# A two-layer decoder trunk on one core: gated GEMM steps and RWKV chain batches tied in turn, a first norm from raw rows, group-norm turns moved later

## The chip, the cores and the metric

The kernel runs on one core of a Trainium2 chip. The metric is the device time of one execution in microseconds (us), as the median of several runs. The engines are named as in the profile: PE is TensorE (PEld its weight loads), DVE VectorE, ACT ScalarE, POOL GpSimd, and SP the engine that here issues nearly all the weight DMAs.

## The reference

Two layers on 256 tokens of width 1024. Each layer is a half-step SwiGLU FFN (inner width 2816), two mixers side by side with gates, and a second half-step FFN; a last RMS norm ends it. Cut to what the change touches:

```python
for layer in range(2):
    x = x + 0.5 * swiglu_ffn(rms_norm(x, ffn1_norm[layer]), ...)
    h = rms_norm(x, mix_norm[layer])
    p = h @ w_in
    y_a = chunked_sgu(...)                    # gMLP spatial gating
    # RWKV-7, per head and token t (64x64 state):
    #   sa = state @ kk_t
    #   state = state * w_t - sa (kk_t a_t)^T + v_t k_t^T
    #   y_t = state @ r_t, then group norm per head, gain, bias, + bonus
    y_b = rwkv7_time_mix(...)
    merged = sigmoid(gate_a) * (y_a @ w_proj_a) + sigmoid(gate_b) * (y_b @ w_proj_b)
    x = x + merged @ w_out
    x = x + 0.5 * swiglu_ffn(rms_norm(x, ffn2_norm[layer]), ...)
out = rms_norm(x, final_norm)
```

## The kernel before

**GEMMs.** Every large product is done in three products of halves, since the operands are split into a rounded high part and a rest: high by high, high by low and low by high (L236, L237, L238), 128x512 outputs in PSUM. A weight unit is 128x2x512 (512 KB): SP loads it (L206, tile `wr`), ACT casts the high half (L220, `wh`), DVE subtracts the low half (L221, `wl`). Three raw buffers and four split buffers let this run a few units ahead of PE. One unit feeds 12 matmuls, or 2 token blocks x 2 k tiles x 3 products. Whatever PE does, it does in the order in which the program left it; the same holds for ACT, DVE, POOL and SP.

**The mixer stage.** In each layer `mixers` first computes the projections that RWKV needs, then the gMLP branch, and then the part that the change is about:

1. `rwkv_inverse`: DVE inverts triangular 32x32 blocks row by row (L819 and L821 in turn, then two block transposes L823 and L824). PE meanwhile runs gated GEMMs.
2. `rwkv_offdiag`: 32x32 matmuls that join the blocks (L836 and L854, 128 each), with ACT and DVE copies between (L840, L845, L859).
3. `rwkv_chain`: four chunks c = 0 to 3 of 64 tokens, each a chain of batches of small matmuls: products of the keys with the values (L884), with the state (L895), an ACT copy (L899), the inverse applied (L905), an ACT copy (L909), the new state's terms (L924), and on DVE the new state (L929, L930, at c = 0 L932). After c = 1 and c = 3 the outputs y of 128 tokens come from L942 and L950; ACT copies them (L956). 
4. `rwkv_scale`, the group norm of these y: ACT squares (L969), DVE reduces (L971), POOL makes the inverse root (L972, L973), DVE scales (L974). `rwkv_turn`: POOL loads a bias term (L984), PE transposes (L988), ACT applies gain and bias (L992), DVE adds (L994), ACT casts the high half (L996), DVE subtracts the low half (L997). It runs for each of two head groups g and token halves tb.
5. `y @ w_proj_b` by `chunk_a` (two halves of 48 matmuls), merged by L1037 and L1038 and transposed (L318), then `w_out`.

Beside steps 1 to 4, `gated` supplies 24 GEMM steps of 12 matmuls (8 for gate a, 8 for `y_a @ w_proj_a`, 8 for gate b) with ACT's tanh (L1062) and DVE's merge (L1069). `weave` takes one step and then one batch of the chain in turn:

```python
while more:
    next(fill, None)
    with self.tc.issue_after(self.last_mm):
        more = next(steps, steps) is not steps
```

So a batch stands behind the last matmul of the step before it. The steps themselves are held by nothing: the scheduler places their matmuls where its own clock finds PE free, which is often in the middle of a batch and, most of all, ahead of the first one, while DVE inverts.

**The start.** x arrives in two loads, one on SP and one on ACT, the norm's gain is broadcast to 128 rows by SP; DVE multiplies x by the gain (L344) and ACT squares x (L343); PE transposes the product (L318), ACT and DVE split it (L322, L323).

Of the kernel before, what the change touches and what calls it, by code (L numbers as in the profile page):

```python
# [36 lines left out]
class Trunk:  # L37
# [77 lines left out]

    def layer_vectors(self, l):
# [83 lines left out]
    def pump(self):  # L200
        nc = self.nc
        with self.tc.high_priority(offset=2000):
            while self.n_load < min(len(self.units), self.n_used + RAW_BUFS + HL_BUFS - 1):
# [36 lines left out]
    def chunk_a(self, x, token_first):  # L240
# [94 lines left out]

    def norm_half(self, tb, j, g):
# [6 lines left out]
        nc.scalar.activation(self.tt([P, 512]), x, AF.Square, scale=1.0 / 32, accum_out=self.ss[tb][:, j:j + 1])  # L343
# [27 lines left out]
    def ffn(self, l, n, ht, before, after, aside=None):  # L371
# [4 lines left out]
        rf = self.rf  # L376
# [13 lines left out]
        for ci, c in enumerate(self.gu_order):  # L390
            ps = self.chunk_a(ht, ci == 0)
# [6 lines left out]
            if c0 < dff:  # L398
                t = self.zt([P, NTB, 512])
                gates[c] = t  # L400
                for tb in range(NTB):
                    nc.scalar.activation(t[:, tb, :g1 - c0], ps[tb][:, :g1 - c0], AF.Silu, scale=rf[tb])
            if u0 < c1:
# [4 lines left out]
                for tb in range(NTB):  # L408
                    s = lo
                    while s < hi:  # L410
# [3 lines left out]
                                                       rf[tb], gates[gc][:, tb, s - 512 * gc:e - 512 * gc],  # L414
# [46 lines left out]
    def load_x(self, queues):  # L461
        self.x = [self.wt([P, D]) for _ in range(NTB)]
        for tb in range(NTB):
            queues[tb].dma_start(self.x[tb], self.xsrc[tb])
# [362 lines left out]
    def rwkv_offdiag(self, grs, T, Tt, Tn):  # L827
# [3 lines left out]
        for h in range(2):  # L831
            ps = [self.mp().rearrange("p (u s) -> p u s", s=32) for _ in range(2)]
            for u in range(16 * h, 16 * h + 16):
                for g in range(2):
                    r0, r1 = slice(64 * g, 64 * g + 32), slice(64 * g + 32, 64 * g + 64)
                    nc.tensor.matmul(ps[g][r1, u - 16 * h, :], lhsT=grs[g]["G"][u // 8][r0, u % 8, 32:64],  # L836
# [12 lines left out]
        for h in range(2):  # L849
            ps = [self.mp().rearrange("p (u s) -> p u s", s=32) for _ in range(2)]  # L850
            for u in range(16 * h, 16 * h + 16):
                for g in range(2):
                    r0, r1 = slice(64 * g, 64 * g + 32), slice(64 * g + 32, 64 * g + 64)
                    nc.tensor.matmul(ps[g][r0, u - 16 * h, :], lhsT=pb[r1, u, :], rhs=Tt[r1, :, u],  # L854
# [7 lines left out]
    def rwkv_chain(self, st, grs, scale, turn):  # L862
# [9 lines left out]
        mm = nc.tensor.matmul  # L872
# [17 lines left out]
        for c in range(4):  # L890
# [21 lines left out]
            if c == 2:  # L912
                for g in range(2):
                    turn(g, 0, ys[g])
# [43 lines left out]
        yield  # L958
        yield
        for g in range(2):  # L960
            turn(g, 1, ys[g])
# [38 lines left out]
    def mixers(self, l, ht, before, after):  # L1000
# [21 lines left out]
        fill = self.gated(ht, yaT, ms)  # L1022
        self.weave(self.rwkv_offdiag(grs, *blocks), fill)
# [8 lines left out]
        for j in range(2):  # L1032
            ps = self.chunk_a(ybT, j == 0)
# [39 lines left out]
    def build(self):  # L1073
# [11 lines left out]
        def before(vec, scaled=False):  # L1085
            def f(first=False):
                state["scaled"] = scaled
                if first:
                    self.load_x((nc.sync, nc.scalar))
                self.g = self.bcast(vec, self.wt, nc.sync if first else nc.gpsimd)  # L1090
                state["ht"] = None
                if not first:
                    self.load_x((nc.gpsimd, nc.gpsimd))
# [12 lines left out]
        with self.tc.high_priority(offset=8000):  # L1106
            before(a["ffn1_norm"][0])(True)
            self.first_consts()
            self.norm_begin()
            for tb in range(NTB):  # L1110
                for j in range(2):
                    self.norm_half(tb, j, self.g)
                after(tb)
# [7 lines left out]
        for l in range(self.depth):  # L1121
            self.ffn(l, "ffn1", state["ht"], before(a["mix_norm"][l], True), after, None if l else tables)
# [3 lines left out]
            else:  # L1126
                self.ffn(l, "ffn2", state["ht"], before(a["final_norm"]), last)

# [32 lines left out]
```

## Time and profile before

| | before |
|---|---|
| median of 3 runs | 1450.06 us (1449.78 to 1453.37) |
| the profiled execution | 1450.86 us, its span 1449.2 us |
| PE busy | 1377.2 us, 95% of the span |
| DVE / ACT / POOL busy | 62% / 51% / 10% |
| mean granted PE clock | 0.986 of full speed |

The span is the time between the first and the last instruction of the profiled execution; 1.7 us lie around it. In the rows, a line such as `L836` is a line of this kernel, `out<-in` gives the tiles by name, and a bracket such as `[1.77 <-DVE w L824]` says how long the engine stood idle before that row and what released it. Busy times of single matmuls overlap (0.39 us each where a new one starts every 0.23 us), so a matmul's cost on PE is the distance between starts.

### The profile page before, as it was taken

The numbers are of one execution on the slowest core, as the hardware profiler recorded it, in microseconds if no ns is written. First come the engines' busy times: TensorE is split into PE (matmuls) and PEld (weight loads), VectorE is DVE, ScalarE is ACT, GpSimd is POOL, SyncE is SP. The second block draws the span as 40 slices with busy tenths as digits, with TensorE's granted clock in tenths as the row PEclk, the third lists the DMA queues.
The fourth block names the chain that finished last, engine by engine and source line by source line (L and its number), as shares of the span: only waits on it lengthen the run. The fifth ranks groups of instructions, "written<-read, shape, count | busy, mean of one in ns | idle before, by whom it ended". The sixth has DMA issues, their size and how long they took to land. (4 is left out here: it accounts for less than half of the span.)

```text
span 1449.2 us, 21790 instructions
## 1 busy us (share of the span) xinstructions
PE 1377.2 (95%) x8642; PEld 1155.3 (80%) x8642; DVE 894.7 (62%) x1216; ACT 735.6 (51%) x1033; POOL 138.2 (10%) x200
## 2 busy tenths in 40 slices
PE   6999999999899999999999999999988989999996
PEld 5888879887787778888888888898867767788885
DVE  4555466769874565555555554769788636555553
ACT  5444456646555545444454443765655545545442
POOL 5000011113102110000010000110140011100000
PEclk9999999999989999999999999999999899999999
DMA  7755557443443567665576655674434425665552
GB/s 230 236 185 190 179 174 239 145 140 117 148 144 88 189 212 230 188 188 181 185 260 188 189 180 187 198 224 134 145 117 145 132 74 189 225 208 180 189 187 88
DMA packets 116871, 254.64 MB, mean 176 GB/s; under 512 B 8878, under 2 KB 12096, under 8 KB 116768
## 3 DMA queue, kind: packets, MB, share of 16 engines
q1 hardware_dynamic: 108048, 226.00, 48.7%
q0 software_dynamic: 8576, 26.72, 5.5%
q8 instruction: 68, 1.11, 0.3%
q10 hardware_dynamic: 144, 0.52, 0.1%
q14 instruction: 35, 0.29, 0.1%
HBM read 243.77 MB, written 9.44 MB: 175 GB/s over the span
## 5 line engine op out<-in xcount | busy, mean ns | idle before, releaser
L221 DVE TENSOR_TENSOR wl<-wr,wh 128x1024 fp32r<-128x1024 f32 x427 | 523.0, 1227 | 392.2 <-ACT wh L220 388.2
L220 ACT CAST wh<-wr 128x1024 fp32r<-128x1024 f32 x427 | 448.5, 1052 | 507.6 <-PE g L238 388.9
L236 PE MATMUL g<-wh,z 128*128 128x512 f32 x1088 | 431.5, 397 | 2.4 <-ACT z L322 2.4
L238 PE MATMUL g<-wh,z 128*128 128x512 f32 x1088 | 430.4, 396 | 3.3 <-DVE z L323 3.3
L237 PE MATMUL g<-wl,z 128*128 128x512 f32 x1088 | 429.2, 394 | 0.5 <-DVE wl L221 0.5
L238 PEld LDWEIGHTS g<-wh,z 128*128 128x128 f32 x1088 | 205.7, 189 | 48.5 <-DVE z L323 6.4
L236 PEld LDWEIGHTS g<-wh,z 128*128 128x128 f32 x1088 | 206.1, 189 | 45.2 <-ACT z L322 4.1
L237 PEld LDWEIGHTS g<-wl,z 128*128 128x128 f32 x1088 | 206.0, 189 | 43.2 <-DVE wl L221 1.7
L236 PE MATMUL g<-wh,w 128*128 128x512 f32 x416 | 162.9, 392 | 0.0
L237 PE MATMUL g<-wl,w 128*128 128x512 f32 x416 | 162.2, 390 | 0.0
L238 PE MATMUL g<-wh,w 128*128 128x512 f32 x384 | 149.7, 390 | 0.0
L296 PE MATMUL g<-z,wh 128*128 128x256 f32 x384 | 109.5, 285 | 0.0
L297 PE MATMUL g<-z,wl 128*128 128x256 f32 x384 | 109.3, 285 | 0.0
L294 PE MATMUL g<-z,wh 128*128 128x256 f32 x384 | 108.9, 284 | 0.0
L237 PEld LDWEIGHTS g<-wl,w 128*128 128x128 f32 x416 | 78.1, 188 | 15.8
L236 PEld LDWEIGHTS g<-wh,w 128*128 128x128 f32 x416 | 78.1, 188 | 15.7
L238 PEld LDWEIGHTS g<-wh,w 128*128 128x128 f32 x384 | 72.1, 188 | 14.9
L297 PEld LDWEIGHTS g<-z,wl 128*128 128x128 f32 x384 | 73.6, 192 | 0.5 <-issue 0.5
L296 PEld LDWEIGHTS g<-z,wh 128*128 128x128 f32 x384 | 73.7, 192 | 0.2 <-issue 0.2
L294 PEld LDWEIGHTS g<-z,wh 128*128 128x128 f32 x384 | 73.6, 192 | 0.2 <-issue 0.2
L318 PE MATMUL m<-ident,z 128*128 128x128 f32 x336 | 50.8, 277 | 17.0 <-DVE z L344 8.4
L472 POOL DMA_DIRECT2D xspill<-w x10 | 5.7, 574 | 601.7 <-DVE w L456 601.7
(232 smaller groups left out, 1256.0 us busy)
## 6 DMA issues: line engine op xcount, KB each, us to landing
wr<-in_ffn_w_gu_dram SPq DMA_DIRECT2D x176, 512.0 KB, 3.6
wr<-in_ffn_w_down_dram SPq DMA_DIRECT2D x88, 512.0 KB, 3.5
wr<-in_w_in_rest_dram SPq DMA_DIRECT2D x58, 512.0 KB, 3.5
wr<-in_w_in_first_dram SPq DMA_DIRECT2D x57, 512.0 KB, 4.0
wr<-in_w_proj_a_dram SPq DMA_DIRECT2D x16, 512.0 KB, 3.7
wr<-in_w_proj_b_dram SPq DMA_DIRECT2D x16, 512.0 KB, 3.7
wr<-in_w_out_dram SPq DMA_DIRECT2D x16, 512.0 KB, 4.0
xspill<-w POOLq DMA_DIRECT2D x10, 512.0 KB, 3.3
```

Source lines behind the costliest of these rows:

```text
L220: nc.scalar.copy(hi, raw)
L221: nc.vector.tensor_tensor(lo, raw, hi.bitcast(F32), ALU.subtract)
L236: mm(ps, lhsT=xh, rhs=wh, start=first, stop=False)
L237: mm(ps, lhsT=xh, rhs=wl, start=False, stop=False)
L238: self.last_mm = mm(ps, lhsT=xl, rhs=wh, start=False, stop=last).ins
L294: mm(o, lhsT=hi[:, k, cs], rhs=xh[kt // 4][:, kt % 4, :], start=(kt == 0 and b % 2 == 0), stop=False, skip_group_check=True)
L296: mm(o, lhsT=hi[:, k, cs], rhs=xl[kt // 4][:, kt % 4, :], start=False, stop=False, skip_group_check=True)
L297: mm(o, lhsT=lo[:, k, cs], rhs=xh[kt // 4][:, kt % 4, :], start=False, stop=kt == NK - 1, skip_group_check=True)
L318: nc.tensor.transpose(ps[:, i * P:(i + 1) * P], src[:, i * P:(i + 1) * P], self.ident)
L472: self.nc.gpsimd.dma_start(self.xsrc[tb], self.x[tb])
```

## The change

- **Both sides tied.** Each gated step that is taken during the weave is put behind the last small matmul of the batch before it (`last_small`); the batch was behind the step already. Small matmuls now go through the helper `small` (all at L1116 of the new program).
- **Eleven steps held back.** Of the 24 gated steps 13 (`FREE_STEPS`) are taken ahead of the weave and are free; the other 11 come only between batches.
- **Turns moved.** The turn of the first token half, which was taken inside chunk c = 2, comes after the whole chain; that of the second half, which followed the chain, is called from inside `y @ w_proj_b` (`between=(2, self.late)`), after the third unit's products for the first token block.
- **First norm.** PE transposes the raw rows of x; the gain is applied on the way out of PSUM (ACT for the high half, DVE for the low half), from a column of gains that is itself transposed from an 8x128 load. x comes in halves on SP and ACT, the second token block's halves behind the first block's casts. The squares come after the second block's transposes, which stand after the first unit's GEMMs (`between=(0, rest)`).
- Later reloads of x go by POOL's queue, as they did.

```diff
+    def first_norm(self, vec, xt):
+        rows = self.cp.tile([NK, P], F32, name="grows")
+        nc.sync.dma_start(rows, vec.rearrange("(k p) -> k p", p=P))
...
+                r.append(q.dma_start(self.x[tb][:, js], self.xsrc[tb][:, js]))
...
+                    nc.tensor.transpose(ps[:, k, :], self.x[tb][:, (4 * j + k) * P:(4 * j + k + 1) * P], self.ident)
...
+                    hi = nc.scalar.activation(part(0, k), ps[:, k, :], AF.Identity, scale=g(k))
...
+                    lo = nc.vector.scalar_tensor_tensor(part(1, k), ps[:, k, :], g(k), part(0, k).bitcast(F32),
+                                                        ALU.mult, ALU.subtract)
...
+        with behind(first), behind(hi), behind(lo):
+            self.pump(2)
+            load(1)
...
+            hi, lo = turn(1)
+            with behind(hi):
+                for tb in range(NTB):
+                    for j in range(2):
+                        self.square(tb, j)
+                    self.rf[tb] = self.norm_factor(tb, "rf")
...
@@ chunk_a @@
                 go(0, us[i], 2 * i)
+                if between and between[0] == i:
+                    with self.tc.issue_after(self.last_mm):
+                        between[1]()
...
@@ rwkv_chain @@
-            if c == 2:
-                for g in range(2):
-                    turn(g, 0, ys[g])
...
+            if c == 1:
+                early = ys
         for g in range(2):
-            turn(g, 1, ys[g])
+            turn(g, 0, early[g])
+        self.late = lambda: [turn(g, 1, ys[g]) for g in range(2)]
...
@@ mixers @@
         fill = self.gated(ht, yaT, ms)
+        for _ in range(FREE_STEPS):
+            next(fill)
+        self.last_small = None
         self.weave(self.rwkv_offdiag(grs, *blocks), fill)
...
-            ps = self.chunk_a(ybT, j == 0)
+            ps = self.chunk_a(ybT, j == 0, None if j else (2, self.late))
...
@@ weave @@
-            next(fill, None)
+            if self.last_small is None:
+                next(fill, None)
+            else:
+                with self.tc.issue_after(self.last_small):
+                    next(fill, None)
...
+    def small(self, *args, **kw):
+        r = self.nc.tensor.matmul(*args, **kw)
+        self.last_small = r.ins
+        return r
...
+FREE_STEPS = 13
```

How the instructions move is shown at three places. The rows give the line, the operation, the output and input tiles with buffer numbers, and the shape.

**DVE at the end of the inverse of layer 2.** `nr` and `w` are the inverse's row products and blocks, `wl` a weight unit's low half, `z` a merged gate. Before, the last rows up to the second transpose:

```order
L221 TENSOR_TENSOR wl_10612<-wr_10532,wh_10611 128x1024
L821 TENSOR_TENSOR w_9687<-w_9687,nr_9768 128x5x27
L1069 SCALAR_TENSOR_TENSOR z_10228<-z_10228,g_10530 128x512
L819 TENSOR_TENSOR nr_9771<-w_9685,w_9687 128x112
L1069 SCALAR_TENSOR_TENSOR z_10228<-z_10228,g_10531 128x512
L221 TENSOR_TENSOR wl_10716<-wr_10569,wh_10715 128x1024
L821 TENSOR_TENSOR w_9687<-w_9687,nr_9771 128x4x28
L819 TENSOR_TENSOR nr_9774<-w_9685,w_9687 128x87
L821 TENSOR_TENSOR w_9687<-w_9687,nr_9774 128x3x29
L819 TENSOR_TENSOR nr_9777<-w_9685,w_9687 128x60
L821 TENSOR_TENSOR w_9687<-w_9687,nr_9777 128x2x30
L819 TENSOR_TENSOR nr_9780<-w_9685,w_9687 128x31
```

Four more rows follow there: one more `wl`, L821, L823 and L824. In the changed kernel the same stretch, down to the transposes (L881 and L882, which were L823 and L824):

```order
L879 TENSOR_TENSOR w_9711<-w_9711,nr_9792 128x5x27
L877 TENSOR_TENSOR nr_9795<-w_9709,w_9711 128x112
L879 TENSOR_TENSOR w_9711<-w_9711,nr_9795 128x4x28
L877 TENSOR_TENSOR nr_9798<-w_9709,w_9711 128x87
L879 TENSOR_TENSOR w_9711<-w_9711,nr_9798 128x3x29
L877 TENSOR_TENSOR nr_9801<-w_9709,w_9711 128x60
L879 TENSOR_TENSOR w_9711<-w_9711,nr_9801 128x2x30
L877 TENSOR_TENSOR nr_9804<-w_9709,w_9711 128x31
L879 TENSOR_TENSOR w_9711<-w_9711,nr_9804 128x31
L881 STREAM_TRANSPOSE w_9692<-w_9711 128x1024
L882 STREAM_TRANSPOSE w_9709<-w_9711 128x1024
```

The three `wl` and two merges of a gate that stood among these rows are gone from the stretch. Over the whole inverse of layer 2 that leaves twelve `wl` where fifteen stood.

**DVE around the last states of layer 1.** `state` are the chain's states, `gv` and `t` the group norm's sums and values, `t_4165` and `t_4590` loaded bias terms. Before, the states of c = 1, then the group norm of the first token half, its turn, and the first row of the state of c = 2:

```order
L929 TENSOR_TENSOR state_3985<-m_3976,state_3845 128x256
L930 TENSOR_TENSOR state_3985<-state_3985,ec_1821 128x256
L929 TENSOR_TENSOR state_3997<-m_3988,state_3856 128x256
L930 TENSOR_TENSOR state_3997<-state_3997,ec_1821 128x256
L971 TENSOR_REDUCE gv_4073<-t_4071 128x8
L974 TENSOR_TENSOR t_4068<-t_4068,gv_4073 128x512
L971 TENSOR_REDUCE gv_4083<-t_4081 128x8
L221 TENSOR_TENSOR wl_4445<-wr_4316,wh_4444 128x1024
L974 TENSOR_TENSOR t_4078<-t_4078,gv_4083 128x512
L994 TENSOR_TENSOR t_4071<-t_4071,t_4165 128x512
L997 TENSOR_TENSOR w_3714<-t_4071,w_3712 128x4x128
L929 TENSOR_TENSOR state_4220<-m_4211,state_3985 128x256
```

In the changed kernel the group norm of the first half (L1027 and L1030, which were L971 and L974) stands ahead of the states of c = 2 (L984 and L985, which were L929 and L930):

```order
L1027 TENSOR_REDUCE gv_4344<-t_4342 128x8
L1030 TENSOR_TENSOR t_4339<-t_4339,gv_4344 128x512
L1027 TENSOR_REDUCE gv_4354<-t_4352 128x8
L1030 TENSOR_TENSOR t_4349<-t_4349,gv_4354 128x512
L273 TENSOR_TENSOR wl_4381<-wr_4211,wh_4380 128x1024
L984 TENSOR_TENSOR state_4448<-m_4439,state_4256 128x256
L985 TENSOR_TENSOR state_4448<-state_4448,ec_1845 128x256
L984 TENSOR_TENSOR state_4460<-m_4451,state_4268 128x256
L985 TENSOR_TENSOR state_4460<-state_4460,ec_1845 128x256
```

Behind these come the group norm of the second half and only then the turn of the first half (L1050 and L1053, which were L994 and L997):

```order
L1027 TENSOR_REDUCE gv_4575<-t_4573 128x8
L1027 TENSOR_REDUCE gv_4585<-t_4583 128x8
L1030 TENSOR_TENSOR t_4570<-t_4570,gv_4575 128x512
L1030 TENSOR_TENSOR t_4580<-t_4580,gv_4585 128x512
L1050 TENSOR_TENSOR t_4342<-t_4342,t_4590 128x512
L1050 TENSOR_TENSOR t_4352<-t_4352,t_4604 128x512
L1053 TENSOR_TENSOR w_3986<-t_4342,w_3984 128x4x128
L1053 TENSOR_TENSOR ld_3987<-t_4352,w_3985 128x4x128
```

The state of c = 2 (`state_4448`, `state_4460`) now waits on DVE for both scalings of the first half, and the first half's turn (`t_4342<-t_4342,t_4590`) for both scalings of the second half.

**PE between the chain's last batch and `y @ w_proj_b`, layer 1.** L1044 are the turn's transposes (L988 before). Before, gated GEMMs (`z` on the right) stand around the second half's turn; ten of them lie between its two groups of transposes, of which the first is seen here:

```order
L237 MATMUL g_4441<-wl_4423,z_1588 128x512
L238 MATMUL g_4441<-wh_4422,z_1590 128x512
L236 MATMUL g_4545<-wh_4444,z_1587 128x512
L237 MATMUL g_4545<-wl_4445,z_1587 128x512
L988 MATMUL m_4462<-ident,t_4400 128x128 x4
L238 MATMUL g_4545<-wh_4444,z_1589 128x512
L236 MATMUL g_4545<-wh_4444,z_1587 128x512
L237 MATMUL g_4545<-wl_4445,z_1587 128x512
```

In the changed kernel the last of the chain is followed by one group of transposes and the first matmul of `y @ w_proj_b` (`w_3984` is the first half's turned y):

```order
L1116 MATMUL m_4504<-state_4268,w_2980 64x64
L1116 MATMUL m_4505<-state_4268,w_2980 64x64
L1116 MATMUL m_4504<-state_4460,w_2980 64x64
L1116 MATMUL m_4505<-state_4460,w_2980 64x64
L1044 MATMUL m_4592<-ident,t_4339 128x128
L1044 MATMUL m_4606<-ident,t_4349 128x128 x4
L288 MATMUL g_4624<-wh_4173,w_3984 128x512
L289 MATMUL g_4624<-wl_4174,w_3984 128x512
L290 MATMUL g_4624<-wh_4173,w_3986 128x512
L288 MATMUL g_4624<-wh_4173,w_3984 128x512
L289 MATMUL g_4624<-wl_4174,w_3984 128x512
```

No gated GEMM is left behind the chain; the first half's three transposes of group 0 stand already among the last batch.

## Rows read from the trace of the kernel before

**Rows 1.** The page: busy shares (us, share of the span, instructions)

```profile
PE 1377.2 (95%) x8642; PEld 1155.3 (80%) x8642; DVE 894.7 (62%) x1216; ACT 735.6 (51%) x1033; POOL 138.2 (10%) x200
```

**Rows 2.** Windows: length, busy of PE, PEld, DVE, ACT, POOL, clock, DMA share

```profile
422.13:511.05 88.92, 82.79 (x1148) 67.21 (x1149) 42.45 (x59) 47.85 (x95) 15.67 (x19) 0.94 0.40 130
1141.79:1225.93 84.14, 77.29 (x1110) 61.85 (x1111) 37.84 (x55) 45.20 (x93) 12.25 (x15) 0.88 0.35 112
1142.00:1155.66 13.66, 13.66 (x295) 11.69 (x289) 5.03 (x10) 9.55 (x20) 0.00 (x0) 0.50 0.25 81
```

**Rows 3.** Timeline of PE, both layers: start, length, row [idle before <-releaser]

```profile
384.05 0.47 PE L238 MATMUL g<-wh,z 128*128 128x512 f32 x1
...
419.99 0.39 PE L237 MATMUL g<-wl,z 128*128 128x512 f32 x1
422.13 0.56 PE L836 MATMUL m<-w,w 32*32 32x32 f32 x14 [1.75 <-DVE w L824]
...
1141.79 0.40 PE L836 MATMUL m<-w,w 32*32 32x32 f32 x8 [1.77 <-DVE w L824]
```

**Rows 4.** Timeline of DVE near the end of layer 2's inverse

```profile
1134.13 0.68 DVE L1069 SCALAR_TENSOR_TENSOR z<-z,g 128x512 f32<-128x512 f32 x1
...
1137.35 1.22 DVE L221 TENSOR_TENSOR wl<-wr,wh 128x1024 fp32r<-128x1024 f32 x1
1138.48 0.18 DVE L821 TENSOR_TENSOR w<-w,nr 128x31 f32<-128x31 f32 x1
```

**Rows 5.** Timeline of PE in the chains of both layers

```profile
426.58 4.30 PE L854 MATMUL m<-w,w 32*32 32x32 f32 x128
...
436.44 1.35 PE L924 MATMUL m<-w,bk 128*64 128x64 f32 x32
...
443.71 2.13 PE L942 MATMUL m<-w,w 128*64 128x64 f32 x64
...
1171.92 1.30 PE L905 MATMUL m<-t,w 64*64 64x64 f32 x32 [0.21 <-ACT t L899]
...
1177.74 1.09 PE L988 MATMUL m<-ident,t 128*128 128x128 f32 x4 [3.40 <-DVE t L974]
...
1182.11 0.63 PE L236 MATMUL g<-wh,z 128*128 128x512 f32 x1
1182.53 0.60 PE L237 MATMUL g<-wl,z 128*128 128x512 f32 x1
...
1193.97 1.16 PE L950 MATMUL m<-state,w 64*64 64x64 f32 x64
```

**Rows 6.** Timeline of ACT behind layer 2's last L950

```profile
1195.18 0.65 ACT L956 COPY t<-m 128x256 f32<-128x256 f32 x2 [3.33 <-PE m L950]
1195.86 0.63 ACT L969 ACTIVATE t<-t 128x512 f32<-128x512 f32 x1
...
1206.31 0.62 ACT L996 CAST w<-t 128x512 fp32r<-128x512 f32 x1
```

**Rows 7.** The same stretch on DVE, then on POOL

```profile
1196.52 0.69 DVE L971 TENSOR_REDUCE gv<-t 128x8 f32<-128x512 f32 x1 [7.54 <-ACT t L969]
...
1199.28 0.69 DVE L974 TENSOR_TENSOR t<-t,gv 128x512 f32<-128x512 f32 x1 [2.08 <-POOL gv L973]
...
1197.58 1.67 POOL L973 TENSOR_TENSOR gv<-gv,mhalf 128x8 f32<-128x8 f32 x1
1199.22 1.59 POOL L984 DMA_DIRECT2D t<-bspill  x2
```

**Rows 8.** Timeline of the start, ACT and PE

```profile
5.43 0.63 ACT L343 ACTIVATE t<-w 128x512 f32<-128x512 f32 x1 [2.92 <-DMA w<-in_x_dram]
...
8.40 1.94 PE L318 MATMUL m<-ident,z 128*128 128x128 f32 x8 [8.40 <-DVE z L344]
...
11.79 0.80 PE L236 MATMUL g<-wh,z 128*128 128x512 f32 x1 [1.46 <-ACT z L322]
...
20.46 0.39 PE L236 MATMUL g<-wh,z 128*128 128x512 f32 x1
```

More of the change, by code (lines that the diff above doesn't have):

```diff
@@ L114, in consts, with load, turn, rest @@
         self.vec, self.omm, self.omka, self.hka = [], [], [], []
+    def first_norm(self, vec, xt):
+        nc = self.nc
+        rows = self.cp.tile([NK, P], F32, name="grows")
+        nc.sync.dma_start(rows, vec.rearrange("(k p) -> k p", p=P))
+        self.x = [self.wt([P, D]) for _ in range(NTB)]
+        def load(tb):
+            r = []
+            for j, q in enumerate((nc.sync, nc.scalar)):
+                js = slice(512 * j, 512 * j + 512)
+                r.append(q.dma_start(self.x[tb][:, js], self.xsrc[tb][:, js]))
+            return r[0].ins
+        def turn(tb):
+            for j in range(2):
+                ps = self.mp().rearrange("p (k t) -> p k t", t=P)
+                for k in range(4):
+                    nc.tensor.transpose(ps[:, k, :], self.x[tb][:, (4 * j + k) * P:(4 * j + k + 1) * P], self.ident)
+                part = lambda p, k: xt[p][j][:, k, tb * P:tb * P + P]
+                g = lambda k: gain[:, 4 * j + k:4 * j + k + 1]
+                for k in range(4):
+                    hi = nc.scalar.activation(part(0, k), ps[:, k, :], AF.Identity, scale=g(k))
+                for k in range(4):
+                    lo = nc.vector.scalar_tensor_tensor(part(1, k), ps[:, k, :], g(k), part(0, k).bitcast(F32),
+                                                        ALU.mult, ALU.subtract)
+            return hi.ins, lo.ins
+        behind = self.tc.issue_after
+        first = load(0)
+        self.first_consts()
+        ps = self.mp()[:, 0:NK]
+        nc.tensor.transpose(ps, rows, self.ident[0:NK, 0:NK])
+        gain = self.cp.tile([P, NK], F32, name="gain0")
+        nc.vector.tensor_copy(gain, ps)
+        hi, lo = turn(0)
+        with behind(first), behind(hi), behind(lo):
+            self.pump(2)
+            load(1)
+        self.norm_begin()
+        def rest():
+            hi, lo = turn(1)
+            with behind(hi):
+                for tb in range(NTB):
+                    for j in range(2):
+                        self.square(tb, j)
+                    self.rf[tb] = self.norm_factor(tb, "rf")
+        return rest
     def layer_vectors(self, l):
@@ L238, in mm3, with chunk_a @@
         self.last_mm = mm(ps, lhsT=xl, rhs=wh, start=False, stop=last).ins
-    def chunk_a(self, x, token_first):
+    def chunk_a(self, x, token_first, between=None):
         xh, xl = x
@@ L334, in norm_begin, with square @@
         self.rf = [None] * NTB
+    def square(self, tb, j):
+        self.nc.scalar.activation(self.tt([P, 512]), self.x[tb][:, 512 * j:512 * j + 512], AF.Square, scale=1.0 / 32,
+                                  accum_out=self.ss[tb][:, j:j + 1])
     def norm_half(self, tb, j, g):
@@ L342, in norm_half @@
         x = self.x[tb][:, js]
-        nc.scalar.activation(self.tt([P, 512]), x, AF.Square, scale=1.0 / 32, accum_out=self.ss[tb][:, j:j + 1])
+        self.square(tb, j)
         nc.vector.tensor_tensor(self.h[tb][:, js], x, g[:, js], ALU.mult)
@@ L368, in norm_finish, with ffn @@
             self.transpose_split(h[:, 512 * j:512 * j + 512], xt[0][j], xt[1][j], tb)
-    def ffn(self, l, n, ht, before, after, aside=None):
+    def ffn(self, l, n, ht, before, after, aside=None, between=None):
         nc, dff = self.nc, self.dff
@@ L375, in ffn @@
         aT = []
-        rf = self.rf
         def put_act(t, k0, k1):
@@ L390, in ffn @@
         for ci, c in enumerate(self.gu_order):
-            ps = self.chunk_a(ht, ci == 0)
+            ps = self.chunk_a(ht, ci == 0, None if ci else between)
             turn()
@@ L401, in ffn @@
                 for tb in range(NTB):
-                    nc.scalar.activation(t[:, tb, :g1 - c0], ps[tb][:, :g1 - c0], AF.Silu, scale=rf[tb])
+                    nc.scalar.activation(t[:, tb, :g1 - c0], ps[tb][:, :g1 - c0], AF.Silu, scale=self.rf[tb])
             if u0 < c1:
@@ L871, in rwkv_chain @@
         nc = self.nc
-        mm = nc.tensor.matmul
+        mm = self.small
         TTm = nc.vector.tensor_tensor
@@ L1106, in build @@
         with self.tc.high_priority(offset=8000):
[L1107 to L1113, printed above, removed]
+            state["ht"] = self.ht()
+            rest = self.first_norm(a["ffn1_norm"][0], state["ht"])
         self.pump()
@@ L1121, in build @@
         for l in range(self.depth):
-            self.ffn(l, "ffn1", state["ht"], before(a["mix_norm"][l], True), after, None if l else tables)
+            self.ffn(l, "ffn1", state["ht"], before(a["mix_norm"][l], True), after, None if l else tables,
+                     None if l else (0, rest))
             self.mixers(l, state["ht"], before(a["ffn2_norm"][l]), after)
```

25 lines of the change are left out of this document (10 added, 15 removed).

## The prediction

> **What bounds the kernel now.** I read the page first: PE is busy 95% of the span, no other engine above 62% [rows 1], so whatever adds PE idle time or PE time at the low clock adds to the end. Then the windows of the stage that the change rewrites, from the first small matmul of a layer's chain to the first matmul of `w_out`: 88.92 us in layer 1 and 84.14 in layer 2, at a mean granted clock of 0.94 and 0.88 [rows 2]. Then PE's timeline. Gated GEMMs run without a gap before the chain, 159 of them from 384.05 to 419.99 in layer 1, which makes 0.227 us each [rows 3]; at half clock they start 0.42 to 0.43 apart [rows 5]. PE then waits only 1.75 and 1.77 us for DVE's last transpose [rows 3]: the GEMMs cover the inverse. In the chain its largest wait is 3.40 us, for the group norm [rows 5]. [...]
>
> **The wait ahead of the chain.** 11 of 24 steps leave the stretch before the first batch, but some stood behind it before. From the order: 168 gated matmuls stand ahead of the first batch where 188 stood in layer 1 (20 fewer, 20 x 0.227 = 4.5 us) and, in layer 2, 142 in the last run where 200 stood (58 fewer, 13.2 us). In layer 2 DVE loses three low-half splits, 1.13 us from start to start, and two merges of at most 0.68, about 0.6 [rows 4], so its inverse ends 3.4 + 1.2 = 4.6 us sooner; in layer 1 only one 0.4 us copy moves behind it. PE's wait becomes 1.75 + 4.5 - 0.4 = 5.8 us in layer 1 and 1.77 + 13.2 - 4.6 = 10.4 in layer 2. The chain begins at 421.7 and 1137.2 in place of 422.13 and 1141.79. Nothing can fill these waits: the steps that would are behind small matmuls now. The bounds are narrow, since PE's order is fixed: 1 us either way.
>
> **The chain with clean steps.** I lay the new order of PE out from the first small matmul. L836 and L854: 128 matmuls each, 4.30 us for one such batch at the low clock [rows 5] and about 3.8 for the smaller, 8.1 together; 12 GEMMs between them at half clock 12 x 0.427 = 5.1; the 24 behind them 5.4. That is 18.6. Then 84 GEMMs in 7 runs of 12, 19.1 us, alternate with batches: three L884 of 1.15, two L905 of 1.30, two L924 of 1.35, two L895 of 0.7, and L942 with L950 at 2.13 and 1.16 [rows 5]; L884 and L895 I take at the rate of L905 or a little below, which makes 13.4 us. Sum 51.1. A run of 12 lasts 2.7 us, so copies between batches, 0.65 and 1.30 on ACT [rows 6] (L909 has four of the copies that L956 has in pairs), are covered there.
>
> **The uncovered end of the chain.** After the last run nothing stands between the batches: L905, L884, L924, L895, L905, L942, L950, 9.2 us of PE. Their waits come bare: about 0.55 for the value copies, 0.7 and 0.8 for the copies around L895 and L905. The state that c = 3 needs now stands on DVE behind both scalings of the first token half, each of which waits for a reduce (0.69), POOL's root (1.67, with L972 ahead of it 1.9) and itself takes 0.69 [rows 7], and behind one 1.13 split. From the last L950 of c = 1: copies and square 1.3 to 1.9, reduce 0.6, POOL 1.9, scale 0.6, the second pair 0.6 + 1.9 + 0.6, split 1.1, two states 1.8, some 10.5 in all; PE has 0.7 + 2.7 + 1.3 + 1.15 + 0.55 + 1.35 = 7.7 to do meanwhile. I take a wait of 2.9; bounds 0 and the 3.40 that the group norm cost before [rows 5]. With it 14.2, running sum 65.3.
>
> **The gap before y.** This is the largest new term. `y @ w_proj_b` needs the first half's turn. On DVE that turn stands behind both scalings of the second half, and these begin only when the last L950 is out. Counted from its end: ACT copies, one turn activation, and squares, 0.65 + 0.46 + 0.63, then the second group's, 3.2 in all [rows 6]; DVE's first reduce done at 2.45. POOL: L972, then a bias load whose issue takes half of 1.59, the root 1.67, a second load's issue, L972 and a second root [rows 7], done at 7.95. DVE: scaling 0.6, add 0.6; ACT's cast 0.62 [rows 6]; with the hops 9.95. PE has 0.7 us of transposes to set against it, where before gated GEMMs stood there. Bounds: 1.8 (what the covered wait for the inverse was [rows 3], if the order cost next to nothing) and 12. Running sum 75.3.
>
> **y itself.** 96 matmuls of 0.227. Behind the wait of 3.40 GEMMs start 0.42 apart [rows 5]; after a gap of 10 the clock will be down too, and I price 12 at half clock, 5.1, and 84 at full, 19.1. Transposes 1.9 (four groups of four, each at about half of the 1.09 that they took at the low clock [rows 5]), 0.3 until the low half is there, 1.7 for the late turn's own activation, add and cast that the fourth unit waits for: 28.1. Sum 103.4, and 1.3 for the hand-over between 64-row and 128-row matmuls at some ten places: C = 105. Of this 83 us would be left at full clock without a wait.
>
> **The layers.** Layer 1: 421.7 + 105 - 511.05 = +15.6. Layer 2: 1137.2 + 105 - 1225.93 = +16.3.
>
> **The start.** x's gain multiply leaves DVE's path and the four squares leave ACT's path to the first cast: 4 x 0.63 = 2.5 us [rows 8]. PE's transposes need x alone, so they begin near 4.7 in place of 8.40; the first GEMM needs the casts and comes at about 9.7 in place of 11.79. I take -2.5. Bounds: 0, since the second block's half of x is issued by ACT behind two casts and may come late, and -4.5. The other turns of the diff (x reloads on POOL, which they used already) cost nothing as they lie beside 95% busy PE.
>
> In the rows the clock is at its full level by 20.46, 12.1 us after the first transposes and 8.7 after the first GEMM [rows 8]. [...]
>
> **The sum.** 15.6 + 16.3 - 2.5 = +29.4 on the profiled execution's 1450.86 us (span 1449.2 and 1.7 around it), that is 1480.3; it lies 0.8 above the median, so 1479 as a median.
>
> **Rivals.**
> *Milder.* The same new waits, but smaller: the state of c = 3 is not late (2.9), POOL's load issues do not hold up its roots (1.6), the clock is up again in y and in the first GEMM run (2.5 and 2): 9 us less per layer, 1479 - 18 = 1461. For it: the ends of small batches overlap on PE, so that a wait may be smaller than the sum of its parts. Against it: the DVE order leaves no way around the scalings.
> *Worse.* With PE half idle from the last run on, the low clock stays to the middle of y: 9 us of batches nearly double in part (+4), 24 more GEMMs at half clock (+5): about +10 per layer, 1499. For it: the clock of 0.50 for 13.66 us on end behind the first batches [rows 2]. Against it: in the chain's later part L905 took 1.30 before, at the full clock [rows 5].
> *Faster.* Whole runs of 12 keep the clock up and end the splitting of GEMMs by small matmuls, and the waits that matter vanish beneath them. Before, windows of 88.92 and 84.14 hold 6 to 9 us of idle PE and 4 and 7 us of lost clock (88.92 - 82.79, 84.14 - 77.29, and the clock) [rows 2]. If C fell to the 83 to 84 of clean work, each layer would end 5 to 6 us sooner, with the start -13.5: 1436. The point from which it decides is the gap before y: with C below 88 the layers gain, and C below 88 needs a gap under some 2 us and a state that is in time. The DVE order speaks against both.
> *No change.* Recovered clock and idle time (some 28 us) and the new waits cancel: 1450. That the new order does not take hold can be left out: the order on all engines differs as the diff says.
>
> **Chances.** Forecast 0.63 (1468 to 1490 by its own bounds), milder 0.17, worse 0.11, faster 0.05, no change 0.04. About 0.3% is what a measurement of this kernel tells from no change. Faster 0.05, same 0.04, slower 0.91. The range leaves out the faster case, no change and the upper half of worse: 1458 to 1498.
>
> **What would show it.** In the changed profile: PE's wait before the first 32x32 batch of 5 to 7 and 9 to 12 us, released by DVE's second transpose (L882); a wait of 8 to 11 us before the first matmul of y, released by ACT's cast of the first half (L1052); one of 2 to 4 us before L1116 with a state, released by DVE L984 or L985; the windows from first batch to `w_out` near 105 us; the first GEMM near 9.7 us. The forecast is wrong if y's first matmul comes within 3 us of the last L1116, or if these windows are under 95 us.

## The result: slower by 2.4%, and the profile after

The changed kernel takes 1485.57 us (median of 4 runs, 1483.51 to 1487.71) beside 1450.01 of the kernel before on the same chip: ratio 1.0238, 95% interval 1.0224 to 1.0252. The forecast was 1479, with a range of 1458 to 1498. The profiled execution took 1483.51 us, the shortest of the four; against the 1450.86 of before that is +32.7, where the working gave +29.4.

The page of the changed kernel, span and busy shares, answers to [rows 1]. PE is busy 5.8 us longer than before and idle 26.7 us longer:

```profile
span 1481.7 us, 21807 instructions
PE 1383.0 (93%) x8643; PEld 1161.6 (78%) x8643; DVE 896.1 (60%) x1225; ACT 737.0 (50%) x1045; POOL 134.4 (9%) x200
```

The windows from the first batch to the first `w_out` matmul in both layers (columns as in [rows 2]: length, busy time of five engines, clock, DMA share). They took 88.92 and 84.14 us before:

```profile
420.16:524.90 104.74, 89.31 (x1169) 73.21 (x1169) 42.96 (x60) 47.77 (x95) 14.29 (x19) 0.89 0.34 112
...
1153.34:1258.56 105.22, 89.78 (x1168) 73.62 (x1169) 43.06 (x60) 48.97 (x97) 12.19 (x15) 0.89 0.32 103
```

Both are 105 us long now. Their content is nearly equal, since the same 120 gated matmuls stand in either.

PE's largest waits, first as sums over the whole program (total us, times, longest), then as rows of its timeline (start, length, row, idle time before it). They answer to [rows 3] and to the waits for L988 in [rows 5]:

```profile
PE g L288 <- ACT w L1052: 21.9, 4, 9.6
PE m L1116 <- DVE w L882: 16.6, 2, 10.8
PE m L1116 <- DVE state L985: 7.4, 4, 3.2
```

```profile
414.01 0.39 PE L290 MATMUL g<-wh,z 128*128 128x512 f32 x1
420.16 1.06 PE L1116 MATMUL m<-w,w 32*32 32x32 f32 x31 [5.76 <-DVE w L882]
...
469.61 0.39 PE L290 MATMUL g<-wh,z 128*128 128x512 f32 x1
...
485.70 1.16 PE L1116 MATMUL m<-state,w 64*64 64x64 f32 x64
486.79 0.76 PE L1044 MATMUL m<-ident,t 128*128 128x128 f32 x5
497.16 0.79 PE L288 MATMUL g<-wh,w 128*128 128x512 f32 x1 [9.61 <-ACT w L1052]
...
507.22 0.50 PE L288 MATMUL g<-wh,w 128*128 128x512 f32 x1 [1.33 <-ACT w L1052]
...
1153.34 3.83 PE L1116 MATMUL m<-w,w 32*32 32x32 f32 x128 [10.83 <-DVE w L882]
...
1210.20 0.33 PE L1116 MATMUL m<-state,w 64*64 64x64 f32 x4 [3.23 <-DVE state L985]
1211.00 0.68 PE L1116 MATMUL m<-state,w 64*64 64x64 f32 x28 [0.46 <-DVE state L985]
...
1230.66 0.79 PE L288 MATMUL g<-wh,w 128*128 128x512 f32 x1 [9.60 <-ACT w L1052]
1231.26 0.63 PE L289 MATMUL g<-wl,w 128*128 128x512 f32 x1
1231.68 0.63 PE L290 MATMUL g<-wh,w 128*128 128x512 f32 x1
```

PE runs dry at 414.4 and waits 5.76 us for the inverse; in layer 2 it waits 10.83 us for the same. Behind the last batch, five transposes are all it has before y's first matmul, 9.6 us later in both layers, and y then begins at half clock (granted 0.50 from 497 to 500, 0.42 us from start to start).

Where the 9.6 us go is read from DVE and POOL behind the last L950 of layer 1, which ends at 486.9. They answer to [rows 7]. DVE first:

```profile
488.46 0.69 DVE L1027 TENSOR_REDUCE gv<-t 128x8 f32<-128x512 f32 x1 [11.00 <-ACT t L1025]
489.88 0.69 DVE L1027 TENSOR_REDUCE gv<-t 128x8 f32<-128x512 f32 x1 [0.73 <-ACT t L1025]
492.39 0.69 DVE L1030 TENSOR_TENSOR t<-t,gv 128x512 f32<-128x512 f32 x1 [1.83 <-POOL gv L1029]
495.16 0.69 DVE L1030 TENSOR_TENSOR t<-t,gv 128x512 f32<-128x512 f32 x1 [2.08 <-POOL gv L1029]
495.77 1.29 DVE L1050 TENSOR_TENSOR t<-t,t 128x512 f32<-128x512 f32 x2
```

```profile
489.24 0.20 POOL L1028 TENSOR_SCALAR gv<-gv 128x8 f32<-128x8 f32 x1 [15.22 <-DVE gv L1027]
489.81 0.86 POOL L1040 DMA_DIRECT2D t<-bspill  x1 [0.37 <-issue]
490.69 1.66 POOL L1029 TENSOR_TENSOR gv<-gv,mhalf 128x8 f32<-128x8 f32 x1
492.31 0.79 POOL L1040 DMA_DIRECT2D t<-bspill  x1
493.19 0.19 POOL L1028 TENSOR_SCALAR gv<-gv 128x8 f32<-128x8 f32 x1
493.46 1.67 POOL L1029 TENSOR_TENSOR gv<-gv,mhalf 128x8 f32<-128x8 f32 x1
```

The first half's add (L1050) needs nothing of the second half, but stands on DVE behind both scalings of the second half (L1030), which wait for two roots of 1.7 us on POOL, each of them behind a DMA issue of 0.8. ACT's cast follows at 496.5 and PE at 497.16.

The start answers to [rows 8]: transposes and GEMMs of PE.

```profile
4.17 1.97 PE L134 MATMUL m<-ident,w 128*128 128x128 f32 x8 [1.62 <-DMA w<-in_x_dram]
...
8.75 0.79 PE L288 MATMUL g<-wh,z 128*128 128x512 f32 x1 [2.60 <-ACT wh L272]
...
14.79 0.66 PE L134 MATMUL m<-ident,w 128*128 128x128 f32 x4 [1.43 <-DMA w<-in_x_dram]
15.20 0.47 PE L288 MATMUL g<-wh,z 128*128 128x512 f32 x1
...
17.34 0.39 PE L288 MATMUL g<-wh,z 128*128 128x512 f32 x1
```

The row at 17.34 is the 16th GEMM; before, the 16th started at 20.46. So 3.1 us are gained in this execution. Other executions with the same start gain more, less or nothing, as the first experiment shows.

### The profile page after: what moved, and what is told of

Its sections match the earlier page's. It is cut to its first block, busy times and chain, and to the rows that moved or that the text cites. A ratio compares the mean times of both kernels' runs of the same rounds, so it can differ in the third digit from the quotient of the medians.

```text
span 1481.7 us, 21807 instructions
## 1 busy us (share of the span) xinstructions
PE 1383.0 (93%) x8643; PEld 1161.6 (78%) x8643; DVE 896.1 (60%) x1225; ACT 737.0 (50%) x1045; POOL 134.4 (9%) x200
## 5 line engine op out<-in xcount | busy, mean ns | idle before, releaser
L288 PE MATMUL g<-wh,w 128*128 128x512 f32 x416 | 165.3, 397 | 21.9 <-ACT w L1052 21.9
L290 PE MATMUL g<-wh,w 128*128 128x512 f32 x384 | 151.4, 394 | 0.0
```

Source lines behind the costliest of these rows:

```text
L288: mm(ps, lhsT=xh, rhs=wh, start=first, stop=False)
L290: self.last_mm = mm(ps, lhsT=xl, rhs=wh, start=False, stop=last).ins
```

## The experiments

All times are medians; ratios are to the kernel before, run beside each on the same chip, with 95% intervals. Diffs are against the changed kernel where nothing else is said.

**The first norm alone.** The weave, the turns of both halves and the steps are as before the change:

```diff
-            if self.last_small is None:
-                next(fill, None)
-            else:
-                with self.tc.issue_after(self.last_small):
-                    next(fill, None)
+            next(fill, None)
...
-FREE_STEPS = 13
+FREE_STEPS = 0
...
+            if c == 2:
+                for g in range(2):
+                    turn(g, 0, early[g])
```

> Only the first norm from raw rows is kept; the weave, the steps and the turns are those of before. Theory (the start's gain is real and stays to the end, the loss sits in the mixers): 3.0 us less than before, as matmul 16 starts 3.1 us sooner in the changed profile; 1447. Rival (the start's gain is given back by stretches at the low clock further on): within 1 us of before.

Measured: 1451.31, ratio 1.0009 (1.0000 to 1.0017): no gain, the number that the rival named. The trace does not bear out its reason. In this execution the start itself gained nothing: the second block's transposes come at 15.77, and the 16th GEMM starts at 20.52, where it started at 20.46 before and at 17.34 in the changed kernel:

```profile
15.77 1.11 PE L134 MATMUL m<-ident,w 128*128 128x128 f32 x4 [2.02 <-DMA w<-in_x_dram]
...
20.52 0.63 PE L288 MATMUL g<-wh,z 128*128 128x512 f32 x1
```

Eleven kernels here have the new start, the changed one and ten of the experiments. In their profiled executions the 16th GEMM starts anywhere from 15.80 to 20.52. The first GEMM is 2.7 to 3.2 us sooner than before in all of them, but PE's wait for the second block of x is between nothing and 3.21 us, and the first GEMM at the full rate starts between 13.98 and 22.02. The rate is read from the distance of starts, 0.42 against 0.23 us. The clock column of windows of 5 us does not follow it: in these first 25 us it stands at 1.00 before the change and in nine of the eleven, slow rows or not; with no step held it is 0.73 from 15 to 20 and 0.93 from 20 to 25, and with the first half's turn behind the last batch 0.66 from 15 to 20.

Windows far from the start show stretches at the lower clock as well (columns as above, the clock is the third number from the right):

```profile
205.00:225.00 20.00, 17.70 (x91) 15.01 (x92) 13.66 (x16) 11.33 (x16) 2.99 (x4) 0.91 0.54 168
365.00:375.00 10.00, 7.70 (x36) 6.41 (x35) 7.04 (x12) 7.80 (x12) 2.59 (x3) 0.83 0.56 165
1065.00:1095.00 30.00, 24.78 (x151) 20.38 (x150) 22.96 (x43) 18.40 (x29) 7.53 (x7) 0.89 0.41 123
```

Before, none of the three had a low clock; it had one near 320 instead. By windows of 5 us over the whole span, 41 us before and 49 us here lie at the lower level (0.50, the least that a window shows; one of 0.75 counts half); half of the difference is 4 us. The two spans differ by 0.3 us only, so something else in this execution made up for it; what that was is open.

**The turns and the first norm, but no hold and no tie.** The weave's edit is the one above, with the turns left as the change has them.

> Everything of the change but the hold-back and the tie: no step is held, gated steps are free as before; the first norm and the moved turns stay. Theory (hold-back and tie empty the stretch ahead of the chain and uncover its end; the moved turns alone take away the waits for the group norm, 12.3 us in seven places before): waits ahead of the chain back to about 1.8 us, no 9.6 us gap ahead of y, since 74 gated matmuls stand there; 1450 - 3 - 10 = 1437, at most 1445. Rival (the moved turns cost by themselves, through the DVE order that puts the first half's turn behind both scalings of the second half): over 1460, with a gap of 5 us or more ahead of y.

Measured: 1464.56, ratio 1.0099 (1.0081 to 1.0117). My theory missed by 20 us or more. The waits ahead of the chain are 1.8 us, as expected, and in layer 1 the gap ahead of y is filled by 74 gated matmuls. In layer 2 only 28 of them stand there, and PE still waits 4.84 us for the first half's turn. PE's timeline:

```profile
455.10 0.48 PE L1112 MATMUL m<-state,w 64*64 64x64 f32 x4 [3.05 <-DVE state L985]
455.51 0.79 PE L288 MATMUL g<-wh,z 128*128 128x512 f32 x1
456.10 0.63 PE L289 MATMUL g<-wl,z 128*128 128x512 f32 x1
...
492.64 0.79 PE L288 MATMUL g<-wh,w 128*128 128x512 f32 x1 [2.94 <-ACT wh L272]
...
1210.38 0.79 PE L288 MATMUL g<-wh,w 128*128 128x512 f32 x1 [4.84 <-ACT w L1052]
```

In layer 1 the state of c = 2 is 3.05 us late, PE then runs at half clock until about 468 (granted 0.50 from 455 to 465, 0.66 from 465 to 470), and in y a weight unit is late. In layer 2 the state is 2.24 us late. The turns' order on DVE costs by itself, as the rival said.

**States first.** In the changed kernel the first half's group norm is put behind the states of c = 2:

```diff
-                ys.append(scale(y))
+                ys.append(y if c == 1 else scale(y))
...
+            if c == 2:
+                with self.tc.issue_after(done):     # done: the last state of c = 2
+                    early = [scale(y) for y in early]
```

> The changed kernel, but on DVE the states of c = 2 stand ahead of both scalings of the first token half. Theory: the waits of 3.2 and 0.5 us before the small matmuls with a state go in both layers; 5 to 7 us less than the changed kernel, about 1479. Rival (another wait ends last there, a copy on ACT or the group norm's turn): the wait moves to the next batch, less than 2 us gained.

Measured: 1474.50, ratio 1.0158 (1.0144 to 1.0173), 11 us less than the changed kernel, more than either theory gave. The sum of the waits for the state falls from 7.4 us to this:

```profile
PE m L1121 <- DVE state L985: 1.6, 4, 0.5
```

So 5.8 us of waits are worth 11: time at the lower clock falls as well, from 75 to 59 us by windows of 5 us. In the changed kernel some 7 us at the lower level lay behind the late state in each layer (granted 0.77 and 0.54 in the windows of 5 us from 475 to 485, 0.66 in both from 1210 to 1220); here there are none. The windows of layer 1, the changed kernel's first, then this one's:

```profile
470.00:487.00 17.00, 12.51 (x293) 10.67 (x294) 4.63 (x8) 4.74 (x14) 2.52 (x3) 0.80 0.10 33
...
470.00:485.00 15.00, 11.70 (x302) 9.60 (x300) 6.05 (x10) 7.90 (x22) 4.22 (x4) 1.00 0.13 41
```

**No step held.** `FREE_STEPS = 24` in the changed kernel, so that nothing stands between batches.

> The changed kernel with all 24 gated steps free and none between batches. Theory (a held step that only fills a covered place earns no more than it costs ahead of the chain): the waits of 5.8 and 10.8 us ahead of the chain shrink to below 3, and 20 to 25 us of waits and low clock appear between the bare batches of the two chains, so that the time is within 10 us of the changed kernel's 1485, to either side. The gap of 9.6 us ahead of y stays. Rival (the clean runs of 12 between batches are what makes the changed kernel slow): 1465 or less.

Measured: 1474.08, ratio 1.0161 (1.0146 to 1.0176), 11.5 us less than the changed kernel: the theory's bound is missed by 1.5, the rival's by 9. The waits ahead of the chains are gone altogether; the windows of the two chains show the price of bare batches:

```profile
444.68:524.95 80.27, 63.17 (x1049) 54.40 (x1049) 29.11 (x42) 35.20 (x80) 14.31 (x19) 0.81 0.31 99
1171.45:1252.06 80.61, 63.08 (x1050) 54.23 (x1049) 29.49 (x42) 35.73 (x81) 12.21 (x15) 0.81 0.28 91
```

They hold 17 us of idle PE each, 9.6 of it still ahead of y, and a clock of 0.81. Even so this kernel beats the one whose eleven steps cover batches and are paid for ahead of the chain.

**The tie undone, the hold-back kept.** Only the weave's `issue_after(self.last_small)` is taken out of the changed kernel.

> The changed kernel with 11 steps still taken one to a batch, but without the tie behind the last small matmul of the batch before: the scheduler may move a step's matmuls ahead of that batch. Theory (the hold-back, not the tie, makes the wait ahead of the chain and the bare end): only the first steps move ahead of the chain, about 19 matmuls, 4.3 us off its wait in layer 1 and as much in layer 2; the first batches run bare instead; the gap ahead of y stays at 9.6 and the time within 8 us of 1485. Rival (the tie is the cause): under 1465.

Measured: 1475.43, ratio 1.0176 (1.0145 to 1.0206). In medians it is 10 us less than the changed kernel, 2 more than my bound; by the ratios it is 9, and the four executions spread from 1473 to 1484. In layer 1, 20 matmuls move ahead of the chain, and in layer 2, where I expected as many, it is 58. That is as many as stood there before the change, and PE now waits this little for the inverse:

```profile
418.35 1.87 PE L1112 MATMUL m<-w,w 32*32 32x32 f32 x60 [1.52 <-DVE w L882]
...
1151.71 3.80 PE L1112 MATMUL m<-w,w 32*32 32x32 f32 x128 [1.76 <-DVE w L882]
```

So the hold-back does not empty that place: the tie keeps the scheduler from filling it. I had put the wait down to the hold-back alone. The gap ahead of y stays, 9.61 and 9.62 us: with 13 steps taken ahead of the weave, none is left for that place, tie or not. A weave with the tie and no step taken ahead was not run.

**The first half's turn ahead.** States first as above, steps held and tied, and the first half's turn called in chunk c = 3, ahead of the second half's group norm:

```diff
             yield
+            if c == 3:
+                for g in range(2):
+                    turn(g, 0, early[g])
```

> The changed kernel (steps held and tied) with the states of c = 2 first on DVE, as in the run that took 1474.5, and the first half's turn called ahead of the second half's group norm, in chunk c = 3. Theory (the gap ahead of y is the first half's turn behind both scalings of the second half): the wait of 9.6 us goes in both layers, and 4 to 6 us of it come back where PE meets the late turn after 24 matmuls of y; with the clock kept up in y's first matmuls 12 to 16 us less than 1474.5, 1458 to 1462. Rival (the second half's turn is needed so soon that the gap only moves behind y's first unit): within 4 us of 1474.5.

Measured: 1471.66, ratio 1.0157 (1.0144 to 1.0171). In medians that is 3 us less than the run with the states first, which ran on another chip; by the ratios, 1.0157 beside 1.0158, it is nothing. The rival holds. PE's timeline in layer 1:

```profile
481.36 1.08 PE L1050 MATMUL m<-ident,t 128*128 128x128 f32 x4 [3.04 <-DVE t L1036]
...
495.54 1.09 PE L1050 MATMUL m<-ident,t 128*128 128x128 f32 x4 [2.74 <-DVE t L1036]
```

No gap is left ahead of y, but PE meets the transposes of both halves too soon. With no gated matmul at hand, the group norm's latency comes out in one place or another.

**Free steps, early turn later.** No hold, no tie, states first, the first half's turn in c = 3, the second half's as before the change.

> Weave and late turn as before the change (no hold, no tie), first norm from raw rows, states of c = 2 ahead of the first half's group norm, and the first half's turn in chunk c = 3 in place of c = 2. Theory (before, PE reached the first half's transposes 0.8 to 3.4 us too soon, and layer 2's low clock around 1180 followed from that): 6 us of waits and 2 of clock less than the run with the first norm alone, 1443. Rival (the chain has no cover left, so PE waits as long for something else): 1449 or more.

Measured: 1447.33, ratio 0.9984 (0.9974 to 0.9993): half of the gain expected. PE still waits at the early transposes (0.57 and 1.76 us in layer 1, 2.67 in layer 2).

**Both turns later.** The same with the second half's turn inside y.

> As the run beside it (early turn in c = 3, states first, no hold, no tie), and also the second half's turn inside y as in the changed kernel. Theory: the four waits of 1.3 to 1.6 us for the second half's scalings go as well, 6 us less again, 1437. Rival (in y PE meets the late turn, or the weight units come late beside POOL's reloads, as in the run with only the turns moved): not under the run beside it.

Measured: 1444.63, ratio 0.9964 (0.9950 to 0.9977). The moved late turn is worth some 3 us where free steps stand ahead of it.

**The turns free, states first.** The second experiment with the states of c = 2 ahead of the first half's scalings.

> The run with only the turns and the first norm (1464.6), with the states of c = 2 ahead of the first half's scalings on DVE. Theory (what made that run slow is the state that is 3 us late, and the low clock behind it, 15 us long in layer 1): 5 us of waits and 6 to 8 of clock less, about 1452; the weight units that come late in y stay. Rival (the moved turns are slow for the late weight units, the state's wait is covered elsewhere): 1460 or more.

Measured: 1450.34, ratio 1.0006 (0.9997 to 1.0015), 14 us less than without: the state's place was what made that run slow. Of the 5.3 us of waits for the state none is left, the clock is 1.00 from 448 to 470, and the wait ahead of y in layer 2 falls from 4.84 to 2.51. The late weight units in y stay, here on ACT in layer 1:

```profile
485.05 1.04 ACT L272 CAST wh<-wr 128x1024 fp32r<-128x1024 f32 x1 [6.99 <-DMA wr<-in_w_proj_b_dram]
```

**The first half's turn behind the last batch.** As "both turns later", but the early turn is called behind the last L950 and ahead of the second half's group norm:

```diff
+            if c == 3:
+                for g in range(2):
+                    turn(g, 0, early[g])
             ys = []
```

> As the run that took 1444.6 (no hold, no tie, first norm from raw rows, states first, both turns later), but the first half's turn is called behind the last L950 matmuls and ahead of the second half's group norm, so that six of its eight transposes stand behind the chain with 76 gated matmuls after them. Theory (the remaining waits of 2.3 and 2.7 us in chunk c = 3 are transposes that PE reaches too soon): both go, 4 to 6 us less, about 1440. Rival (POOL's reloads and the weight units then fall together in y, as they did where the turns alone were moved, or the clock gives it back): within 2 us of 1444.6.

Measured: 1443.11, ratio 0.9942 (0.9928 to 0.9957), the best of all. In medians it is only 1.5 us below the run with both turns later (by the ratios 3), so the rival is nearer in size, though its reason did not come: POOL's reloads stand ahead of the last roots here, and PE waits for no weight unit in y. The two waits in chunk c = 3 are gone, but in layer 2 PE now waits for the second half's group norm, inside y:

```profile
1196.49 0.63 PE L1050 MATMUL m<-ident,t 128*128 128x128 f32 x4 [2.51 <-DVE t L1036]
```

The windows of both layers, beside 88.92 and 84.14 before the change:

```profile
423.11:506.57 83.46, 81.55 (x1148) 66.87 (x1149) 42.70 (x59) 46.83 (x95) 16.30 (x19) 0.94 0.45 137
1138.85:1218.22 79.37, 75.88 (x1111) 60.73 (x1111) 38.16 (x55) 44.80 (x93) 14.09 (x15) 0.89 0.36 115
```

**The same with the old start.** x times gain on DVE and the squares first, as before the change.

> The same mixers as the run beside it with the first norm of before (x times gain on DVE, squares first). Theory (the new start's 3.1 us are given back by stretches at the low clock, which fall by chance where PE pauses): within 2 us of the run beside it. Rival (the new start earns its 3 us wherever the clock does not take them): 3 us more than the run beside it.

Measured: 1443.84, ratio 0.9947 (0.9933 to 0.9961), 0.7 us from the run beside it: the new start earns nothing that can be measured, a second time. The theory's number came, but this pair does not show its reason: in the two profiled executions the 16th GEMM starts at 20.46 with the new start and at 19.92 with the old one, so there was no gain to give back.

## Why the prediction was right

Its direction, its range and all three large terms came out. Step by step, for layers 1 and 2:

| step | forecast, us | measured, us |
|---|---|---|
| wait ahead of the chain | 5.8, 10.4 | 5.76, 10.83 |
| wait for the state of c = 2 | 2.9 | 3.23 and 0.46 in either layer |
| gap ahead of y, from the end of the last L950 | 9.95 | 10.3, 10.3 (9.61 and 9.60 of it behind the transposes) |
| wait for the late turn | 1.7 | 1.33, 1.33 |
| first batch to `w_out` (C) | 105 | 104.74, 105.22 |
| first GEMM | 9.7 | 8.75 |
| start | -2.5 | -3.1 at the 16th GEMM |

Only the size was off, by 3.3 us in the profiled execution. At layer 1's first `w_out` matmul the changed kernel is 13.85 us late where 13.1 was forecast: its first batch starts at 420.16 where 421.7 - 2.5 = 419.2 was forecast, behind two stretches at the lower clock near 265 and 370 (granted 0.77 to 0.89 by windows of 5 us, 1.00 before). Another 1.8 us were lost between the layers, where windows of 5 us show clocks of 0.66 near 985 and 1105 that the kernel before did not have there. The sum had no term for that. In medians the forecast is off by 6.6: the median lies 2.1 above the profiled execution here, and 0.8 below it before. The mean clocks of the four executions are 0.975, 0.975, 0.972 and 0.970 at 1483.5, 1484.3, 1487.7 and 1486.8 us, so the two longer ones lie at the lower clocks.

That C came out within 0.3 us is in part luck. In layer 1 the uncovered end of the chain (469.8 to 486.9) took 17.0 us where the sum has 14.2. Against these 2.8 us stand the covered part up to the last run of 12 (420.16 to 469.8), 49.7 where the sum has 51.1, and the 1.3 that the sum adds for hand-overs. For these the prediction names no row; in the changed kernel a run of 12 starts its first GEMM 0.34 us ahead of its second and its last 0.32 ahead of the batch (451.30 and 451.64, 453.93 and 454.25 in one of them), where 0.23 lie between the others, so some 0.2 us a run. The other two terms are close, 10.3 beside 9.95 and 27.7 beside 28.1.

Two readings in the prediction do not come out of its rows, and neither moves the forecast much. Four groups of transposes at half of 1.09 are 2.2 us, not 1.9. The rival "faster" names 6 to 9 us of idle PE and 4 and 7 us of lost clock; [rows 2] give 6.1 and 6.9 idle, and a clock of 0.94 and 0.88 over these lengths loses 5.3 and 10.1.

The step on the start came out in the changed kernel's trace and not as a gain of the program. The prediction took one start time for granted; over eleven profiled executions with this start the 16th GEMM begins between 15.80 and 20.52, where it begins at 20.46 and 19.92 in the two with the old start. In both executions that set the start against the old one, with the same mixers, it is no sooner, and the medians of these pairs differ by 0.6 and 0.7 us, in opposite directions. Whether a start that is sooner would keep its gain to the end is therefore not shown by them. Why the second block of x lands at such different times, and why the GEMMs reach the full rate where they do, was not tested. That place differs too among the eleven kernels that share this start: the first GEMM at the full rate is the 8th in the changed kernel (15.52 us) and the 20th in the one with the first norm alone (22.02).

What the prediction calls the low clock is a granted 0.50 in the trace of before: at L854's batch of 4.30 us (426.58 to 430.88) and at L988's group of 1.09 (1177.70 to 1179.00). The full level that it names for 20.46 is read from the rate of the GEMMs alone: the granted clock there is 1.00 in every window of 5 us from 0 to 25, while the fourth to the thirteenth GEMM start 0.42 to 0.43 us apart. What slows these was not shown.

What the prediction did not see is how the causes divide. It treated hold-back and tie as one. Taking out the tie alone brings 10 us back in medians and takes away the long waits ahead of the chain; the steps taken ahead of the weave leave the gap ahead of y, which stays with the tie out and with all steps ahead; setting all steps ahead brings 11.5, and the free weave of before, with neither hold nor tie, 21. And it priced the late state at its 2.9 us of waiting. With steps held, its place costs 5.5 us per layer, 2.9 of them waits that went and the rest the clock behind them. With free steps it costs 14 in all, unevenly: in layer 1 the wait is 3.05 and 13 us at the lower clock follow, in layer 2 the wait is 2.24 and the clock stays up behind it (granted 1.00 from 1170 to 1205).

The rival "faster" needed a gap of less than 2 us ahead of y and a state in time. The changed kernel has neither. Of the kernels with free steps, the three with the new start that have both in either layer (early turn later, both turns later, early turn behind the last batch) are faster than before, by 0.2, 0.4 and 0.6%, far from the 13.5 us of that rival and without its whole runs of 12. The one with the turns free and the states first still waits 2.5 us ahead of y in layer 2, and is as fast as before.

## What to carry to other kernels

A filler that is made to stand between the batches of a chain is paid for at two places. Tied behind a batch, it cannot move ahead of the chain (waits of 5.8 and 10.8 us here, 1.5 and 1.8 without the tie); and steps taken early are not left for the chain's uncovered end (9.6 us in each layer). Keep it free, and look where the chain's last latency falls. Where an engine works in the program's order, put what the critical chain needs (here the new state, then the first half's turn) ahead of a group norm that waits for a slow engine (POOL's roots of 1.66 and 1.67 us here). And price a wait on a busy PE above its length: here 5.8 us of waits for the state were worth 11, since stretches at the lower clock lay behind them (75 us at the lower level with the waits, 59 without). It is no fixed factor: the waits of 1.58 and 1.57 us near 1200 before the change had no such stretch behind them (granted 1.00 from 1195 to 1220).

## What the runs showed of the hardware that was not expected

The same start takes a different time from one execution to the next: with PE's first instructions alike, the first GEMM at the full rate started between 13.98 and 22.02 us and the 16th between 15.80 and 20.52, in eleven profiled executions. A single trace of a start is therefore no measure of what a change there is worth; the medians of the two pairs that differ in it show no gain (ratios 1.0009 to the kernel before, and 0.9942 beside 0.9947). POOL is taken up for 0.8 us by the issue of each bias load, and its roots wait for that: of the 5.9 us from its first sum term (489.24) to the end of the second root (495.13) two issues took 1.65.
